# Hybrid encoder trunk on one core: small constants merged or moved, S5 eigenvalues first, silu(c) as a row in its own stream

## The chip, the cores and the metric

The kernel runs on one core of a Trainium2 chip. The metric is the device time of one execution in microseconds (us). A run that times a kernel repeats it; the median of the repeats counts. One further execution was recorded by the hardware profiler, and all rows below come from that one.

## The reference, cut to what matters

Two encoder layers are applied to x (512 tokens by 2048 channels, f32), both conditioned on a vector c (2048).

```python
def ada_modulate(x, c, norm_g, ada_w, ada_b):
    mod = silu(c) @ ada_w + ada_b                   # 2048 -> 3 * 2048
    shift, scale, gate = split(mod, 3)
    return rms_norm(x, norm_g) * (1 + scale) + shift, gate

# layer 0
h, gate = ada_modulate(x, c, ...)
q, k, v, g_a, u, g_b = split(h @ w_in)
out = concat(attention(q, k, v) * silu(g_a), s5(u) * silu(g_b)) @ w_out
x = x + gate * out
# layer 1: the same wrapper round a neighbourhood attention and an SSD scan
```

The S5 part needs tables of powers of its eigenvalues (lambda, log step, and a vector of the exponents), the matrices B and C, a diagonal D, and a gated output projection with a bias. All products are f32, built of three passes on a split into a rounded high part and a rest.

## The kernel before, in words

All loads and stores are issued from one queue, SP's. A planner of the kernel framework fixes the order of the instructions on every engine's queue before the run, from the program's order, from priorities (`high_priority`), from when it thinks that each one's inputs are ready, and from `issue_after(ins)`, which keeps an instruction behind another on the same queue without a wait. A load that the program asks for late, but whose buffer is free, can thus stand very early in SP's queue.

`setup` (L905) loads x in eight pieces of 512 KB (L909), then calls `silu_c` (L589), which loads c twice, as columns (`cs`) and as rows (`c_row`), applies silu to both (L599 to L601), and writes the rows to a scratch in DRAM, `cbd` (L602). Then come the identity matrix `ident` (L912) and `mods` (L923), the columns of norms and biases. `s5_params` (L267) loads the eigenvalues `s5_lam` (L277) and the exponents `s5_kx` (L278) and computes the S5 tables step by step, mostly on VectorE (L282 to L361).

`layer0` (L925) then runs 16 rounds k, one for each block of 128 input channels. A round needs four quarters of the adaLN weights, 512 KB each, for block k (`ada_load`, L939, into OLa for even and OLb for odd k) and a 384 KB piece of the input projection (`w_issue`, L142). `ada_sum` (L973, L978, L980) forms shift and scale on TensorE, `ada_cols` (L987 to L992) applies them to x that `x_norm` (L1000) has multiplied by the reciprocal root `rstd` (L651 to L655, from the squares L952 and the sums L956). Then 18 matmuls of the u projection follow (L167 to L169), from round 4 on also 24 of `extra`, with another 512 KB of weights (`w_x`). The quarters of round k + 2 are loaded into the buffer that `ada_sum(k)` has read. `ada_sum(k + 1)` writes the same PSUM bank (b3) from which `ada_cols(k)` reads.

```python
def load_after(self, k):
    return self.tc.issue_after(self.adal[k].ins) if k in self.adal else nullcontext()
```

The S5 matrices C (L498, L499) are queued behind the adaLN quarters of round 4, B (L367) behind those of round 14. Once C is there, the S5 tables of 512 KB each are formed on VectorE (L393 to L397) and written to DRAM (L410).

Later streams run beside the matmuls of the projections, advanced a step at a time by `slot`. `ada_stream` (L604) forms the other modulation vectors on VectorE from 512 KB pieces (L615) and from silu(c), read back from `cbd` and spread over the partitions into `cb` (L624). Small constants are loaded where they are used in the program: `s5dd` (L508, L509) in `s5_kernels`, `bglu` (L1133; scaled on ScalarE, L1134 and L1135) before the GLU matmuls, `tri` and `ssd_rows` (L1201, L1202), `convw` (L1307, scaled on ScalarE L1310), `ssdw` (L1474, scaled on ScalarE L1476), `wqk` (L1499, used on VectorE L1502).

Of the kernel before, what the change touches and what calls it, by code (L numbers as in the profile page):

```python
# [12 lines left out]
AF = mybir.ActivationFunctionType  # L13
ALU = mybir.AluOpType
# [11 lines left out]
HEAD = 1  # L26
PRI_B = 3000
NZ = 6
LK = (-1, 14)
SSLOT = 2  # L30
WB = 3
N0 = 4
# [34 lines left out]
class Trunk:  # L67
# [69 lines left out]
    def w_issue(self, upto, offset=PRI_WD):  # L137
        while self.wi < min(upto, len(self.wq)):
            src = self.wq[self.wi]
            t = self.sl("w", src.shape, bufs=2)  # L140
            with self.tc.high_priority(offset=offset):
                self.wd[self.wi] = self.nc.sync.dma_start(out=t, in_=src)  # L142
            self.wf[self.wi] = t
            self.wi += 1

    def w_prep(self, upto):
        while self.wp < min(upto, len(self.wq)):
# [119 lines left out]
    def s5_params(self, tr, keep, ks):  # L267
# [3 lines left out]

        nc, A = self.nc, self.A
        ev = nc.vector
        w = self.sl(tr[0], [128, 11, 64])
        kx = self.sl("s5kx", [128, 16])
        with self.load_after(ks[0]):
            nc.sync.dma_start(out=w[:, 0:3], in_=A["s5_lam"])  # L277
            nc.sync.dma_start(out=kx, in_=A["s5_kx"])  # L278
        yield
        yield  # L280
        lr, li, dt = w[:, 0], w[:, 1], w[:, 3:11]
        nc.scalar.activation(out=dt[:, 0], in_=w[:, 2], func=AF.Exp)  # L282
        yield
        ev.tensor_tensor(out=dt[:, 1], in0=lr, in1=dt[:, 0], op=ALU.mult)
        ev.tensor_tensor(out=dt[:, 2], in0=li, in1=dt[:, 0], op=ALU.mult)
# [10 lines left out]
        x = self.sl(tr[2], [128, 16, 64])  # L296
# [3 lines left out]
        for c in range(2):  # L300
# [7 lines left out]
            t = self.sl(tr[3], [128, 16, 64])  # L308
# [53 lines left out]
        bb = [self.sl(keep[2 + c], [128, 1024]) for c in range(2)]  # L362
        self.s5_bb = bb
        bt = [self.sl(tr[4 + c], [128, 1024]) for c in range(2)]
        with self.load_after(ks[1]):
            for c in range(2):
                nc.sync.dma_start(out=bt[c], in_=A["s5_b"][:, c])  # L367
        yield
        yield
        for half in range(2):  # L370
            g = slice(half * 32, half * 32 + 32)
# [130 lines left out]
    def s5_kernels(self, ts):  # L502


        nc, A = self.nc, self.A
        self.s5_kk = self.scratch("s5_kk", [16, 128, 240])
        dd = self.sl("s5dd", [128, 2, 16])
        nc.sync.dma_start(out=dd[:, 0], in_=A["s5_dcol"])  # L508
        nc.sync.dma_start(out=dd[:, 1], in_=A["s5_dmask"])  # L509
        w = self.sl(ts[3], [128, 4, 240])  # L510
        cks = {i: self.s5_load_ck(ts[i], i) for i in range(3)}
        yield
        for i in range(16):
# [12 lines left out]
            yield  # L526
            ks = w[:, i % 4]
            nc.scalar.copy(out=ks[:, 0:128], in_=kv[1])
            nc.scalar.copy(out=ks[:, 128:240], in_=kv[0][:, 16:128])
            nc.vector.scalar_tensor_tensor(out=ks[:, 112:128], in0=dd[:, 1], scalar=dd[:, 0, i:i + 1],  # L530
                                           in1=ks[:, 112:128], op0=ALU.mult, op1=ALU.add)
            nc.vector.tensor_tensor(out=ks[:, 112:128], in0=ks[:, 112:128], in1=kv[0][:, 0:16], op=ALU.add)
            nc.sync.dma_start(out=self.s5_kk[i], in_=ks)
            yield
# [51 lines left out]
                nc.sync.dma_start(out=ydram[:, (j - 1) * 4:(j + 1) * 4], in_=y)  # L586
            yield

    def silu_c(self):  # L589

        nc, A = self.nc, self.A
        self.cs = self.sl("cs", [128, 16])
        self.cbd = self.scratch("cbd", [16, 128])
        cr = self.sl("rsq", [16, 2, 128])
        t = self.sl("cst", [128, 16])
        nc.sync.dma_start(out=self.cs, in_=A["c"])
        nc.sync.dma_start(out=cr[:, 0], in_=A["c_row"])
        for x, w in ((self.cs, t), (cr[:, 0], cr[:, 1])):
            nc.scalar.activation(out=w, in_=x, func=AF.Tanh, scale=0.5)  # L599
            nc.vector.scalar_tensor_tensor(out=x, in0=w, scalar=1.0, in1=x, op0=ALU.add, op1=ALU.mult)  # L600
            nc.vector.tensor_scalar(out=x, in0=x, scalar1=0.5, scalar2=None, op0=ALU.mult)  # L601
        nc.sync.dma_start(out=self.cbd, in_=cr[:, 0])  # L602

    def ada_stream(self, groups, tags):  # L604

# [298 lines left out]

    def setup(self):  # L905
        nc, A = self.nc, self.A
        self.xt = [self.sl(f"G{i}", [128, 2, 512]) for i in range(8)]
        for i in range(8):
            nc.sync.dma_start(out=self.xt[i], in_=A["x"].rearrange("(j k p) s -> j p k s", k=2, p=128)[i])  # L909
        self.silu_c()  # L910
        self.ident = self.sl("ident", [128, 128])
        nc.sync.dma_start(out=self.ident, in_=A["ident"])  # L912
        self.ones = self.sl("ones", [128, 1])
        nc.vector.memset(self.ones, 1.0)
        self.epsc = self.sl("epsc", [128, 1])
        nc.vector.memset(self.epsc, EPS)

        self.quad = self.sl("quad", [128, 1])
        nc.vector.tensor_reduce(out=self.quad, in_=self.ident.rearrange("p (a b) -> p b a", b=32)[:, 0], axis=AX.X,
                                op=ALU.add)  # L920

        self.mods = self.sl("mods", [128, 128])
        nc.sync.dma_start(out=self.mods, in_=A["mods"])  # L923

    def layer0(self):  # L925
        nc, A = self.nc, self.A
# [148 lines left out]
        def s5_rest():  # L1075
            yield from self.s5_in([G[14], G[3], G[1], G[2], G[15], G[16], G[17]], st)
            yield from self.qk_tables(("ropeq", "ropek"), G[8])
            a, b = self.s5_scan(st), self.s5_kernels(G[14:18])
            la = lb = True
            while la or lb:  # L1080
                la = la and next(a, "end") != "end"
                lb = lb and next(b, "end") != "end"
                yield
            yield from self.s5_out([G[14], G[15], G[3], G[16], G[10], G[17], G[11], G[0], G[2], G[1]], st, ydram)
        self.start("s5", s5_rest())
        self.sstep = SSLOT
        extra(17)
# [45 lines left out]
        nc.sync.dma_start(out=bglu[:, 0], in_=A["bglu"])  # L1133
# [61 lines left out]
    def dt_stream(self, raw, G):  # L1195
# [2 lines left out]
        v = nc.vector  # L1198
        tri = self.sl(G[13], [128, 3, 128])
        self.tri = tri  # L1200
        nc.sync.dma_start(out=tri[:, 0:2], in_=A["tri"])  # L1201
        nc.sync.dma_start(out=tri[:, 2, 0:80], in_=A["ssd_rows"])  # L1202
# [100 lines left out]
    def conv_stream(self, xins, G, xs):  # L1303

        nc, A = self.nc, self.A
        cw = self.sl("convw", [128, 12, 6])
        nc.sync.dma_start(out=cw, in_=A["convw"])  # L1307
        yield
        yield
        nc.scalar.mul(out=cw, in_=cw, mul=0.5)  # L1310
# [151 lines left out]
    def ssd_end(self, G, ys, z):  # L1462
# [11 lines left out]
        nc.sync.dma_start(out=nw, in_=self.A["ssd_nw"])  # L1474
        yield
        nc.scalar.mul(out=nw, in_=nw, mul=0.5)  # L1476
        for t in range(4):
# [15 lines left out]
    def na_stream(self, T, raws, oc, gdram):  # L1493
# [2 lines left out]
        A = self.A  # L1496
        v = nc.vector
        wqk = self.sl("wqk", [128, 2])
        nc.sync.dma_start(out=wqk, in_=A["o_qkn"])  # L1499
# [321 lines left out]
def host_s5(I):  # L1821
    f = {}
    lre, lim, ls = (np.asarray(I[k])[0] for k in ("s5_lam_re", "s5_lam_im", "s5_log_step"))
    ls = np.broadcast_to(ls[:, :, None], (2, 64, 64))
    f["s5_lam"] = np.stack([a.transpose(0, 2, 1).reshape(128, 64) for a in (lre, lim, ls)], axis=1)
# [7 lines left out]
    for g in range(4):  # L1833
        o = 16 * (g % 2)
        at[0, g, o:o + 16], at[1, g, o:o + 16] = d[g], e[g]
    f["s5_dcol"], f["s5_dmask"] = at.reshape(2, 128, 16)
    j = np.arange(8, dtype=np.float32)
    f["s5_kx"] = np.concatenate([np.repeat(np.concatenate([j + 1, j])[None], 64, 0),
                                 np.repeat(np.concatenate([8 - j, 7 - j])[None], 64, 0)])
    return f  # L1840


def host_layer0(I):
    f = {}
    a = lambda n: np.asarray(I[n])
    f["x"] = a("x")[0].T
    f["c"] = a("c")[0].reshape(16, 128).T
    f["c_row"] = a("c")[0].reshape(16, 128)
    f["ident"] = np.eye(128, dtype=np.float32)
    col = lambda v: v.reshape(16, 128).T  # L1850
    eb, obb = a("e_ada_b")[0], a("o_ada_b")[0]
    f["mods"] = np.concatenate(
        [col(v) for v in (a("e_norm_g")[0], a("o_norm_g")[0], eb[4096:], obb[:2048], obb[2048:4096], obb[4096:],
                          eb[:2048], eb[2048:4096])], axis=1)
# [125 lines left out]
```

## Time and profile before

| | us |
|---|---|
| median of 3 runs | 1838.96 |
| the 3 runs | 1835.25 to 1839.21 |
| the profiled execution's own time | 1831.32 |
| its span, first to last instruction | 1829.5 |
| TensorE busy | 1770.3 (97%) |
| VectorE busy | 1209.7 (66%) |
| ScalarE busy | 730.0 (40%) |
| granted TensorE clock, mean | 0.992 |

Busy is the time in which the engine had at least one instruction running. The time outside the span is 1.8 us. DMA share is the mean busy share of the 16 DMA engines in a stretch (records overlap, so it can read a little over 1), and GB/s is what they moved.

### The profile page before, as it was taken

What the parts mean: (1) busy time and instruction counts of PE and PEld (TensorE: products, weight loads), DVE (VectorE), ACT (ScalarE), POOL (GpSimd) and SP (SyncE); (2) the same over time, 40 slices, a digit from 0 to 9 for tenths busy, and PEclk for the clock granted to TensorE, in tenths of its full rate; (3) what the DMA queues carried; (4) which work ended last, traced back from release to release, by engine and by line L of the source; (5) the groups of instructions that cost most, each with busy time, mean ns of one, the idle gap of its engine ahead of it and who ended that gap; (6) DMA issues with size and microseconds to landing.
All of it is one profiled execution on the core that took longest, in us unless ns stands there. A gap on an engine that the chain in (4) does not pass through costs nothing.

```text
span 1829.5 us, 28824 instructions
## 1 busy us (share of the span) xinstructions
PE 1770.3 (97%) x11176; PEld 1522.8 (83%) x11176; DVE 1209.7 (66%) x2336; ACT 730.0 (40%) x1357; POOL 25.1 (1%) x44
## 2 busy tenths in 40 slices
PE   6899999899999989999999999999999999999999
PEld 3677897699989867888878878878799999997887
DVE  6897697984699999842256676589974453644332
ACT  6333454236235434432243244356644343442211
POOL 0000000000000000011100000000000000000000
PEclk8999999999999989999999999999999999999999
DMA  9997626747989887664435743358533333243542
GB/s 325 375 340 278 186 79 220 241 124 247 313 315 295 285 283 259 209 207 140 138 108 161 246 142 117 104 169 250 165 105 115 110 99 102 93 141 100 180 140 90
DMA packets 140906, 347.52 MB, mean 190 GB/s; under 512 B 31488, under 2 KB 42656, under 8 KB 140768
## 3 DMA queue, kind: packets, MB, share of 16 engines
q1 hardware_dynamic: 140768, 345.67, 57.6%
q8 instruction: 88, 1.44, 0.3%
q14 instruction: 50, 0.41, 0.1%
HBM read 310.48 MB, written 33.56 MB: 188 GB/s over the span
## 4 chain that ended last, share of the span: by engine, by line
PE 65%; DVE 16%; DMA 12%; issue 3%; ACT 1%; SPq 1%; DVEq 0%; ACTq 0%
PE m L167 10%; PE m L169 10%; PE m L168 10%; PE m L235 7%; PE m L234 7%; PE m L236 7%; DMA G<-in_ada_r_dram 6%; DVE G L629 3%; DVE wl L129 3%; PE b L169 2%; PE b L167 2%; PE b L168 2%; PE b L573 1%; PE b L973 1%; PE b L461 1%
## 5 line engine op out<-in xcount | busy, mean ns | idle before, releaser
L129 DVE TENSOR_TENSOR wl<-w,wh 128x1024 fp32r<-128x1024 f32 (+2 forms) x262 | 313.9, 1199 | 256.8 <-ACT wh L128 254.0
L128 ACT CAST wh<-w 128x1024 fp32r<-128x1024 f32 (+2 forms) x262 | 269.1, 1029 | 522.3 <-PE m L168 267.5
L168 PE MATMUL m<-H,wh 128*128 128x512 f32 (+1 forms) x968 | 381.9, 395 | 1.2 <-DVE H L992 1.2
L167 PE MATMUL m<-H,wh 128*128 128x512 f32 (+1 forms) x968 | 380.8, 398 | 2.2 <-ACT G L1144 2.1
L169 PE MATMUL m<-H,wl 128*128 128x512 f32 (+1 forms) x968 | 378.8, 396 | 2.2 <-DVE wl L129 2.2
L234 PE MATMUL m<-wh,H 128*128 128x256 f32 (+2 forms) x1232 | 353.3, 288 | 2.6 <-ACT H L665 1.5
L236 PE MATMUL m<-wh,H 128*128 128x256 f32 (+2 forms) x1232 | 353.8, 289 | 0.3 <-DVE H L1765 0.3
L235 PE MATMUL m<-wl,H 128*128 128x256 f32 (+2 forms) x1232 | 353.0, 287 | 0.2 <-DVE wl L129 0.2
L234 PEld LDWEIGHTS m<-wh,H 128*128 128x128 f32 x1232 | 233.8, 190 | 7.3 <-ACT H L665 2.6
L236 PEld LDWEIGHTS m<-wh,H 128*128 128x128 f32 x1232 | 233.4, 190 | 3.5 <-issue 1.0
L235 PEld LDWEIGHTS m<-wl,H 128*128 128x128 f32 x1232 | 234.0, 190 | 2.6 <-issue 0.7
L167 PEld LDWEIGHTS m<-H,wh 128*128 128x128 f32 x968 | 182.9, 190 | 46.0 <-issue 4.2
L169 PEld LDWEIGHTS m<-H,wl 128*128 128x128 f32 x968 | 181.8, 188 | 44.1 <-issue 3.5
L168 PEld LDWEIGHTS m<-H,wh 128*128 128x128 f32 x968 | 182.3, 188 | 42.4 <-issue 2.6
L629 DVE SCALAR_TENSOR_TENSOR G<-G,cb 128x1024 f32<-128x1024 f32 x128 | 155.0, 1220 | 55.5 <-DMA G<-in_ada_r_dram 47.7
L169 PE MATMUL m<-OLa,wl 128*128 128x512 f32 (+1 forms) x132 | 51.3, 389 | 0.6 <-DVE wl L129 0.5
L167 PE MATMUL m<-OLa,wh 128*128 128x512 f32 (+1 forms) x132 | 51.5, 390 | 0.2 <-ACT wh L128 0.2
L167 PE MATMUL m<-OLb,wh 128*128 128x512 f32 (+1 forms) x132 | 50.1, 388 | 1.4 <-ACT OLb L128 1.4
L167 PE MATMUL b<-H,wh 128*128 128x512 f32 x128 | 50.2, 406 | 0.8 <-DVE G L1045 0.8
L169 PE MATMUL m<-OLb,wl 128*128 128x512 f32 (+1 forms) x132 | 50.9, 386 | 0.0
L168 PE MATMUL m<-OLa,wh 128*128 128x512 f32 (+1 forms) x132 | 50.8, 385 | 0.0
L168 PE MATMUL m<-OLb,wh 128*128 128x512 f32 (+1 forms) x132 | 50.7, 384 | 0.0
(406 smaller groups left out, 2685.2 us busy)
## 6 DMA issues: line engine op xcount, KB each, us to landing
G<-in_ada_r_dram SPq DMA_DIRECT2D x128, 512.0 KB
w<-in_w_kvq_dram SPq DMA_DIRECT2D x72, 512.0 KB
w<-in_w_out_dram SPq DMA_DIRECT2D x64, 512.0 KB
w<-in_w_x_dram SPq DMA_DIRECT2D x36, 512.0 KB
OLa<-in_ada_dram SPq DMA_DIRECT2D x32, 512.0 KB
OLb<-in_ada_dram SPq DMA_DIRECT2D x32, 512.0 KB
G<-s_ck SPq DMA_DIRECT2D x32, 512.0 KB
s_ck<-G SPq DMA_DIRECT2D x16, 512.0 KB
```

The costliest lines, as they stand in the source:

```text
L128: self.nc.scalar.copy(out=hi, in_=src)
L129: self.nc.vector.tensor_tensor(out=lo, in0=src, in1=hi.bitcast(F32), op=ALU.subtract)
L167: mm(out=out, lhsT=lh, rhs=rh, start=start, stop=False)
L168: mm(out=out, lhsT=lh, rhs=rl, start=False, stop=False)
L169: mm(out=out, lhsT=ll, rhs=rh, start=False, stop=stop)
L234: mm(out=o, lhsT=hi, rhs=wh[:, c], start=(k == 0 and i % per == 0), stop=False)
L235: mm(out=o, lhsT=hi, rhs=wl[:, c], start=False, stop=False)
L236: mm(out=o, lhsT=lo, rhs=wh[:, c], start=False, stop=last)
L461: nc.tensor.matmul(out=xp[c][:, gg * 64:gg * 64 + 64], lhsT=gt[:, c, g], rhs=self.s5_u(b * 4 + g))
L573: nc.tensor.matmul(out=yp[:, cols], lhsT=ck[:, c, g], rhs=sts[:, j % 2, c, g], start=False, stop=(c == 1))
L629: nc.vector.scalar_tensor_tensor(out=t, in0=t, scalar=1.0, in1=cb, op0=ALU.mult, op1=ALU.mult, accum_out=o)
L973: nc.tensor.matmul(out=ps[32 * i:32 * i + 32, 0:256], lhsT=self.cs[:, 4 * q + i:4 * q + i + 1].to_broadcast([128, 32]), rhs=abuf[k][:, q, ...
```

## The change

Constants that go together become one input each: identity, `mods` and c as columns are one block of 272 columns, `consts`; the S5 eigenvalues and exponents are one block of 208 columns, `s5_lamk`; the two halves of `s5dd` are one. `s5_lamk` is loaded before anything else, `consts` between the fifth and the sixth piece of x. The silu of c as rows, its store to `cbd` and so the first `cb` move into a stream `silu_row` that starts with the S5 stream after the 16 rounds. `late()` queues a load behind the weight piece issued last in the program: `c_row`, `s5dd`, `bglu`, `tri`, `ssd_rows`, `convw`, `ssdw` and `wqk` get it.

```diff
+    def late(self):
+        return self.tc.issue_after(self.wd[self.wi - 1].ins)
...
 def s5_params
-        w = self.sl(tr[0], [128, 11, 64])
-        kx = self.sl("s5kx", [128, 16])
-        with self.load_after(ks[0]):
-            nc.sync.dma_start(out=w[:, 0:3], in_=A["s5_lam"])
-            nc.sync.dma_start(out=kx, in_=A["s5_kx"])
+        w = self.s5w
...
 def s5_kernels
-        nc.sync.dma_start(out=dd[:, 0], in_=A["s5_dcol"])
-        nc.sync.dma_start(out=dd[:, 1], in_=A["s5_dmask"])
+        with self.late():
+            nc.sync.dma_start(out=dd, in_=A["s5_dd"])
...
-    def silu_c(self):
...
-        nc.sync.dma_start(out=self.cs, in_=A["c"])
-        nc.sync.dma_start(out=cr[:, 0], in_=A["c_row"])
...
+    def silu_row(self):
...
+        with self.late():
+            nc.sync.dma_start(out=cr[:, 0], in_=self.A["c_row"])
+        yield
+        yield
+        self.silu(cr[:, 0], cr[:, 1])
+        yield
         nc.sync.dma_start(out=self.cbd, in_=cr[:, 0])
+        yield
...
 def setup
+        self.s5w = self.sl("G14", [128, 768])
+        nc.sync.dma_start(out=self.s5w[:, 0:208], in_=A["s5_lamk"])
...
+        consts = self.sl("consts", [128, 272])
+        self.ident, self.mods, self.cs = consts[:, 0:128], consts[:, 128:256], consts[:, 256:272]
         for i in range(8):
+            if i == 5:
+                nc.sync.dma_start(out=consts, in_=A["consts"])
             nc.sync.dma_start(out=self.xt[i], in_=...)
-        self.silu_c()
-        nc.sync.dma_start(out=self.ident, in_=A["ident"])
+        self.silu(self.cs, self.sl("cst", [128, 16]))
...
-        nc.sync.dma_start(out=self.mods, in_=A["mods"])
...
 def layer0, after the 16 rounds
+        self.start("crow", self.silu_row())
         self.start("s5", s5_rest())
...
 bglu (and tri, ssd_rows, convw, ssdw, wqk in the same way)
+        with self.late():
+            nc.sync.dma_start(out=bglu[:, 0], in_=A["bglu"])
```

## Rows read from the trace of the kernel before

**Rows 1.** The page's head and its busy table.
```profile
span 1829.5 us, 28824 instructions
PE 1770.3 (97%) x11176; PEld 1522.8 (83%) x11176; DVE 1209.7 (66%) x2336; ACT 730.0 (40%) x1357; POOL 25.1 (1%) x44
```

**Rows 2.** Stretches: length, then busy time of each engine, clock, DMA share, GB/s.
```profile
13.00:20.00 7.00, 5.41 (x26) 1.73 (x24) 6.01 (x17) 6.20 (x11) 0.00 (x0) 1.00 0.92 299
28.00:35.00 7.00, 7.00 (x39) 4.86 (x32) 6.97 (x12) 4.11 (x10) 0.00 (x0) 0.69 0.68 192
35.00:64.00 29.00, 21.76 (x170) 14.87 (x172) 18.93 (x41) 13.46 (x28) 0.00 (x0) 0.98 1.02 401
64.00:70.00 6.00, 6.00 (x38) 3.51 (x36) 6.00 (x11) 2.73 (x4) 0.00 (x0) 0.51 1.01 383
70.00:190.00 120.00, 119.12 (x764) 87.78 (x763) 104.39 (x177) 42.86 (x60) 0.43 (x2) 1.00 0.83 305
200.00:300.00 100.00, 99.44 (x683) 87.58 (x684) 74.58 (x127) 53.50 (x85) 0.00 (x0) 1.00 0.47 133
300.00:400.00 100.00, 91.19 (x926) 75.81 (x912) 96.75 (x337) 24.76 (x51) 0.00 (x0) 1.00 0.63 200
```

**Rows 3.** SP's queue in order of time: start, us, line, transfer, count.
```profile
0.73 4.08 SPq L909 DMA_DIRECT2D G<-in_x_dram  x8
4.86 0.47 SPq L596 DMA_DIRECT2D cs<-in_c_dram  x1
...
11.52 0.33 SPq L278 DMA_DIRECT2D s5kx<-in_s_kx_dram  x1
12.87 2.62 SPq L939 DMA_DIRECT2D OLa<-in_ada_dram  x4
...
19.62 0.33 SPq L142 DMA_DIRECT2D w<-in_w_u_dram  x1
20.89 0.33 SPq L508 DMA_DIRECT2D s5dd<-in_s_dcol_dram  x1
...
28.36 0.32 SPq L602 DMA_DIRECT2D cbd<-rsq  x1
29.28 2.79 SPq L939 DMA_DIRECT2D OLa<-in_ada_dram  x4
...
35.27 0.52 SPq L624 DMA_DIRECT2D cb<-cbd  x1
...
43.48 0.33 SPq L498 DMA_DIRECT2D G<-in_s_c_dram  x1
46.02 0.33 SPq L142 DMA_DIRECT2D w<-in_w_u_dram  x1
```

**Rows 4.** The chain that ended last, 40 to 70 us: start, us, what.
```profile
45.52 0.81 issue
...
53.26 0.49 issue
...
60.38 3.48 issue
63.86 3.64 PE b L973 x32
```

**Rows 5.** VectorE in order of time, in two stretches.
```profile
17.13 2.34 DVE L290 TENSOR_TENSOR G<-G,s5kx 128x1024 f32<-128x1024 f32 x2
...
23.61 0.67 DVE L655 SCALAR_TENSOR_TENSOR r2k<-H,H 128x512 f32<-128x512 f32 x1
...
60.46 0.69 DVE L393 TENSOR_TENSOR H<-G,G 128x512 f32<-128x512 f32 x1
...
63.48 0.22 DVE L987 SCALAR_TENSOR_TENSOR acols<-b,mods 128x1 f32<-128x1 f32 x1
```

**Rows 6.** A GLU weight piece: its issue on SP, its first use on ScalarE.
```profile
614.48 0.33 SPq L142 DMA_DIRECT2D w<-in_w_glu_dram  x1
620.22 1.05 ACT L128 CAST wh<-w 128x1024 fp32r<-128x1024 f32 x1 [1.33 <-DMA w<-in_w_glu_dram]
```

More of the change, by code (lines that the diff above doesn't have):

```diff
@@ L28 @@
 NZ = 6
-LK = (-1, 14)
+LK = 14
 SSLOT = 2
@@ L273, in s5_params @@
         ev = nc.vector
-        w = self.sl(tr[0], [128, 11, 64])
-        kx = self.sl("s5kx", [128, 16])
-        with self.load_after(ks[0]):
-            nc.sync.dma_start(out=w[:, 0:3], in_=A["s5_lam"])
-            nc.sync.dma_start(out=kx, in_=A["s5_kx"])
+        w = self.s5w
         yield
         yield
-        lr, li, dt = w[:, 0], w[:, 1], w[:, 3:11]
-        nc.scalar.activation(out=dt[:, 0], in_=w[:, 2], func=AF.Exp)
+        kx = w[:, 192:208]
+        lr, li, dt = w[:, 0:64], w[:, 64:128], w[:, 256:768].rearrange("p (a g) -> p a g", g=64)
+        nc.scalar.activation(out=dt[:, 0], in_=w[:, 128:192], func=AF.Exp)
         yield
@@ L364, in s5_params @@
         bt = [self.sl(tr[4 + c], [128, 1024]) for c in range(2)]
-        with self.load_after(ks[1]):
+        with self.load_after(ks):
             for c in range(2):
@@ L587, in s5_out, with silu @@
             yield
-    def silu_c(self):
-        nc, A = self.nc, self.A
-        self.cs = self.sl("cs", [128, 16])
+    def silu(self, x, w):
+        nc = self.nc
+        nc.scalar.activation(out=w, in_=x, func=AF.Tanh, scale=0.5)
+        nc.vector.scalar_tensor_tensor(out=x, in0=w, scalar=1.0, in1=x, op0=ALU.add, op1=ALU.mult)
+        nc.vector.tensor_scalar(out=x, in0=x, scalar1=0.5, scalar2=None, op0=ALU.mult)
+    def silu_row(self):
+        nc = self.nc
         self.cbd = self.scratch("cbd", [16, 128])
         cr = self.sl("rsq", [16, 2, 128])
-        t = self.sl("cst", [128, 16])
-        nc.sync.dma_start(out=self.cs, in_=A["c"])
-        nc.sync.dma_start(out=cr[:, 0], in_=A["c_row"])
[L598 to L601, printed above, removed]
+        with self.late():
[4 more added lines that the diff above has]
+        yield
         nc.sync.dma_start(out=self.cbd, in_=cr[:, 0])
+        yield
     def ada_stream(self, groups, tags):
@@ L920, in setup @@
                                 op=ALU.add)
-        self.mods = self.sl("mods", [128, 128])
-        nc.sync.dma_start(out=self.mods, in_=A["mods"])
     def layer0(self):
@@ L1132, in layer0 @@
         bglu = self.sl("bglu", [128, 2, 16])
-        nc.sync.dma_start(out=bglu[:, 0], in_=A["bglu"])
+        with self.late():
+            nc.sync.dma_start(out=bglu[:, 0], in_=A["bglu"])
         nc.scalar.mul(out=bglu[:, 1], in_=bglu[:, 0], mul=0.25)
@@ L1200, in dt_stream @@
         self.tri = tri
-        nc.sync.dma_start(out=tri[:, 0:2], in_=A["tri"])
-        nc.sync.dma_start(out=tri[:, 2, 0:80], in_=A["ssd_rows"])
+        with self.late():
+            nc.sync.dma_start(out=tri[:, 0:2], in_=A["tri"])
+            nc.sync.dma_start(out=tri[:, 2, 0:80], in_=A["ssd_rows"])
         bias, alog, dd = tri[:, 2, 0:32], tri[:, 2, 32:64], tri[:, 2, 64:80]
@@ L1306, in conv_stream @@
         cw = self.sl("convw", [128, 12, 6])
-        nc.sync.dma_start(out=cw, in_=A["convw"])
+        with self.late():
+            nc.sync.dma_start(out=cw, in_=A["convw"])
         yield
@@ L1473, in ssd_end @@
         nw = self.sl("ssdw", [128, 8])
-        nc.sync.dma_start(out=nw, in_=self.A["ssd_nw"])
+        with self.late():
+            nc.sync.dma_start(out=nw, in_=self.A["ssd_nw"])
         yield
@@ L1498, in na_stream @@
         wqk = self.sl("wqk", [128, 2])
-        nc.sync.dma_start(out=wqk, in_=A["o_qkn"])
+        with self.late():
+            nc.sync.dma_start(out=wqk, in_=A["o_qkn"])
         yield
@@ L1824, in host_s5 @@
     ls = np.broadcast_to(ls[:, :, None], (2, 64, 64))
-    f["s5_lam"] = np.stack([a.transpose(0, 2, 1).reshape(128, 64) for a in (lre, lim, ls)], axis=1)
+    lam = np.concatenate([a.transpose(0, 2, 1).reshape(128, 64) for a in (lre, lim, ls)], axis=1)
     b = [np.asarray(I[k])[0].transpose(0, 2, 1, 3).reshape(128, 1024) for k in ("s5_b_re", "s5_b_im")]
@@ L1835, in host_s5 @@
         at[0, g, o:o + 16], at[1, g, o:o + 16] = d[g], e[g]
-    f["s5_dcol"], f["s5_dmask"] = at.reshape(2, 128, 16)
+    f["s5_dd"] = at.reshape(2, 128, 16).transpose(1, 0, 2)
     j = np.arange(8, dtype=np.float32)
-    f["s5_kx"] = np.concatenate([np.repeat(np.concatenate([j + 1, j])[None], 64, 0),
-                                 np.repeat(np.concatenate([8 - j, 7 - j])[None], 64, 0)])
+    kx = np.concatenate([np.repeat(np.concatenate([j + 1, j])[None], 64, 0),
+                         np.repeat(np.concatenate([8 - j, 7 - j])[None], 64, 0)])
+    f["s5_lamk"] = np.concatenate([lam, kx], axis=1)
     return f
@@ L1846, in host_layer0 @@
     f["x"] = a("x")[0].T
-    f["c"] = a("c")[0].reshape(16, 128).T
     f["c_row"] = a("c")[0].reshape(16, 128)
-    f["ident"] = np.eye(128, dtype=np.float32)
     col = lambda v: v.reshape(16, 128).T
     eb, obb = a("e_ada_b")[0], a("o_ada_b")[0]
-    f["mods"] = np.concatenate(
-        [col(v) for v in (a("e_norm_g")[0], a("o_norm_g")[0], eb[4096:], obb[:2048], obb[2048:4096], obb[4096:],
-                          eb[:2048], eb[2048:4096])], axis=1)
+    f["consts"] = np.concatenate(
+        [np.eye(128, dtype=np.float32)] + [col(v) for v in (a("e_norm_g")[0], a("o_norm_g")[0], eb[4096:], obb[:2048], obb[2048:4096], obb[4096:],
+                          eb[:2048], eb[2048:4096], a("c")[0])], axis=1)
     e0, o0 = a("e_ada_w")[0], a("o_ada_w")[0]
```

1 line of the change is left out of this document (removed).

## The prediction

> **What bounds the kernel now.** Read the page's head first: TensorE is busy for 1770.3 of 1829.5 us [rows 1], so 59 us of the span are without a matmul, and a change that touches no matmul can win only there or where the clock is low. The stretches say where that is. From 35 to 64 us TensorE works 21.76 of 29.00 us while the DMA engines are full (share 1.02, 401 GB/s); from 64 to 70 it is busy but at clock 0.51, the level of 1.2 GHz; from 70 to 190 it is busy for 119.12 of 120.00 us with DMA at 0.83, and from 200 to 300 for 99.44 of 100.00 [rows 2]. So the first 64 us are bound by loads, what follows by TensorE, and a load that lands sooner matters until about 64 us.
>
> SP's queue shows how the loads are fed. The eight pieces of x go out in 4.08 us; from there on an issue follows every 1.3 us or so: the loads of 4.86 to 12.87 us are six small ones and the first adaLN quarter, 8.01 us for six steps [rows 3]. 1.33 us is what 512 KB take at 401 GB/s (1.31): each issue waits until the transfer eight places ahead of it has landed. Eight transfers are under way, whatever their size, and when most of them are small the engines run dry. This is seen twice in the stretches: at 13 to 20 us they move 299 GB/s, after the six small loads, and at 28 to 35 us 192, after the seven from 20.89 to 28.36 us, which stand between the weights of round 1 and the quarters of round 2 [rows 2, 3].
>
> The chain of waits in 40 to 70 us shows what TensorE does meanwhile: it waits 0.81 us and 0.49 us at the ends of rounds, then 3.48 us before `ada_sum(5)`, which then runs in 3.64 us at the low clock [rows 4]. The three waits grow as the loads fall behind.
>
> **The change part by part.** All sums are against the profiled execution's 1831.32 us, which is 1.8 us around the span and stands 7.6 us under the median of the three runs (1838.96); the difference found there is carried over to the median.
>
> *The two holes close.* In front of the quarters of round 0 now stand big pieces and two blocks of 104 and 136 KB; between the weights of round 1 and the quarters of round 2 stands nothing. Quarters of round 2 need `ada_sum(0)` done, but behind it a whole round of loads is still under way, so the queue stays full. Against 401 GB/s the holes cost 7.00 x (401 - 299) / 401 = 1.8 us and 7.00 x (401 - 192) / 401 = 3.6 us [rows 2]: 5.4 us.
>
> *`cb` and the small bytes leave.* `cb` (512 KB) goes out at 35.27 us, inside the full stretch. By the rule of eight, the issue at 46.02 us is the one that waited for it, 2.54 us after the one at 43.48 instead of 1.3 [rows 3]. At the full rate its bytes cost 1.3 us, by that spacing at most 2.54; I take 1.5, near the bytes, since other transfers go on meanwhile. The other small loads are 73 KB, 0.2 us.
>
> *What comes in front.* The eigenvalues are issued before x: 4.08 / 8 = 0.5 us of SP's queue ahead of every load. The two blocks hold the bytes that were there before, now ahead of x's end: the last piece of x comes 0.5 + 240 KB / 401 GB/s = 1.1 us later, the quarters behind it 0.5.
>
> Together the loads up to round 5 land 5.4 + 1.5 + 0.2 - 0.5 = 6.6 us sooner.
>
> *VectorE's S5 steps.* With the eigenvalues there at 3 us instead of after 11.52, the first steps run between the squares of x. Now they stand in the way: the pair L290 holds VectorE for 2.34 us from 17.13, and `rstd` ends at 23.61 + 0.67 [rows 5]. The start of the first u matmuls should gain 2 to 3 us in spite of the later x. This adds nothing to the sum while TensorE waits for loads in each round; it makes room: TensorE has 35 to 64 us with 7.2 us idle, so a lead of 6.6 us does not yet make it the bound.
>
> *The clock.* The 6.00 us at 0.51 cost 6.00 x 0.49 = 2.9 us [rows 2]. They follow the wait of 3.48 us; the waits of 0.81 and 0.49 us left the clock at 0.98 in the mean [rows 2, 4]. If TensorE starts 2 to 3 us earlier and the loads come 6.6 us earlier, the waits of four rounds shrink to some 3.5 us in all, below 1 us each, near the short ones. I take the whole 2.9; the other end is 0.
>
> *What is late next.* VectorE: `acols` of round 4 ran at 63.48 us behind a row of S5 steps that began at 60.46 [rows 5], and `ada_sum(5)` needs the bank that it frees. The quarters of round 5 landed just then too, so the row cannot tell which of the two ended the wait. If the planner leaves such a row of steps there, up to 63.48 - 60.46 = 3.0 us of the gain stay away, if not, none; with no row to decide, I take half, 1.5.
>
> *The silu row and `cb`, after round 15.* Three transfers (`c_row`, `cbd`, `cb`), three small operations and two landings that SP waits for in order, now among the S5 loads of u. What hides them is TensorE's queue, 99.44 of 100.00 us, beside a DMA share of 0.47 [rows 2]. Without that cover the price is what `cb` cost at 43.48, 2.54 us [rows 3]. I take 0.
>
> *The late loads* (`s5dd`, `bglu`, `tri`, `ssd_rows`, `convw`, `ssdw`, `wqk`) wait in stages that are not bound by loads. I take 0; the third rival prices them. Merging itself takes instructions from SP's queue alone, which is idle most of the time.
>
> Sum: -6.6 - 2.9 + 1.5 = -8.0 us, from 1831.32 to 1823.3; on the median 1838.96 - 8.0 = **1831.0**.
>
> By rows a small load costs 5.4 us / 13 = 0.4 us in the full stretch. The Trainium skill, "DMA: Bandwidth & Descriptors", in the part on the two cost components, has each transfer pay a fixed 2.0 us or so, mostly for its completion; twelve transfers fewer before 40 us would by that be worth an estimate of 24 us if they came one after another. The rows contradict such a sum, since eight are under way at a time, and I keep to them.
>
> **The rivals.**
>
> *Loads lead, VectorE follows.* VectorE takes over as the bound of the rounds: it is busy for 104.39 of 120.00 us in 70 to 190, and for 96.75 of 100.00 in 300 to 400, the S5 scan [rows 2]. If each round waits for steps put ahead of `acols`, the wait of 3.0 us and the low clock after it stay and the lead is cut again later: 6.6 - 3.0 = 3.6 us at most, and 0 at worst, 1835 to 1839. For it speaks the row of steps before 63.48; against it that S5 work moves into the idle VectorE of the first 15 us, and that TensorE was not held from 70 to 190.
>
> *The change does not open the queue.* The planner may put other loads whose buffers are free into the gap, or keep the weights of round 2 waiting for VectorE's split, so that the next quarters stand behind them: no gain, 1838 to 1840. Against it: after these thirteen the queue holds only loads that need buffers still in use.
>
> *Slower, by late constants on ScalarE.* `bglu`, `convw` and `ssdw` are scaled on ScalarE (L1134, L1310, L1476), now soon after their issue. If ScalarE's queue reaches one before it has landed, the weight casts behind it wait, and TensorE behind those. A load among busy queues takes, as the GLU piece shows, 620.22 - 614.48 = 5.74 us from issue to use [rows 6]; three full waits are 17.2 us, and with the gain of 8.0 the kernel would be 9.2 us slower, 1848. It decides from 8.0 + 3.7 = 11.7 us of waiting on, that is, two of the three in full. For it: ScalarE works through its queue in order. Against it: weights are split two pieces ahead, so TensorE has work for most of such a wait. The Trainium skill, "DMA: Bandwidth & Descriptors", among its rules for kernel authors, advises issuing a load early and waiting for it late; the change does the reverse for seven constants, and by that rule this rival is the one to expect; no row here shows such a late constant yet.
>
> **How the numbers follow.** 0.2% is 3.7 us, about what a measurement of this kernel can tell from no change. The forecast, 5 to 11 us faster, has 0.62. VectorE as the bound has 0.19, of which a quarter still gains over 3.7 us; the unopened queue 0.08, which is no change; late constants 0.11, slower. Faster is 0.62 + 0.05 = 0.67, no change 0.14 + 0.08 = 0.22, slower 0.11. The range: with 2.54 for `cb`, no steps in the way and the whole clock it is 6.6 + 1.0 + 2.9 = 10.5 us, 1828.5; the three runs shown reach 3.7 us under their median, so 1825 is the low end. The high end takes in no change, 1840. Left out are most of the late constants and a little below.
>
> **What would show it.** Right: at 13 to 35 us the DMA engines stay at some 400 GB/s; SP issues the quarters of round 2 some 5 us before 29.28; `ada_sum(5)` starts at about 57 us at the full clock; the 16 rounds end 8 us sooner, and so does each later stage. Wrong: TensorE still waits 3 us before round 5, now for `acols`; a wait at L1134, L1310 or L1476 with weight casts behind it; a new gap between 200 and 300 us behind `cb`; or a lead that is there at the end of the rounds and gone at the end of the S5 stream.

## The result and the profile of the changed kernel

The changed kernel takes 1846.85 us (median of 7 runs, 1842.01 to 1852.55), the kernel before in the same comparison 1835.25 (7 runs, 1830.19 to 1839.21). The ratio is 1.0063, interval 1.0041 to 1.0085: 11.6 us slower, where 8 us faster was forecast. The profiled execution took 1843.35 us, that of before 1831.32.

The page's head and busy table of the changed kernel:

```profile
span 1841.6 us, 28798 instructions
PE 1784.2 (97%) x11176; PEld 1532.5 (83%) x11176; DVE 1208.6 (66%) x2336; ACT 729.3 (40%) x1356; POOL 25.2 (1%) x44
```

Against [rows 1] TensorE's time without a matmul has not grown: 1841.6 - 1784.2 = 57.4 us, before 59.2. The mean granted clock has fallen from 0.992 to 0.987: 1784.2 x 0.013 = 23.2 us lost to it, before 1770.3 x 0.008 = 14.2. These two account for -1.8 + 9.0 = 7.2 of the 12.1 us between the profiles. Stretches show where (columns as in [rows 2]):

```profile
13.00:20.00 7.00, 6.77 (x19) 2.31 (x19) 7.00 (x14) 5.05 (x9) 0.00 (x0) 1.00 1.04 406
28.00:35.00 7.00, 6.88 (x42) 4.00 (x34) 6.22 (x14) 3.81 (x16) 0.00 (x0) 0.87 1.02 402
60.00:64.00 4.00, 2.99 (x25) 1.40 (x26) 4.00 (x9) 2.47 (x3) 0.00 (x0) 0.57 0.59 131
200.00:300.00 100.00, 100.00 (x696) 88.07 (x694) 74.60 (x136) 53.40 (x89) 0.00 (x0) 1.00 0.50 137
300.00:400.00 100.00, 95.30 (x908) 79.03 (x908) 96.07 (x331) 23.20 (x47) 0.00 (x0) 0.95 0.60 192
400.00:480.00 80.00, 77.96 (x562) 73.90 (x562) 35.10 (x65) 44.70 (x84) 0.00 (x0) 0.94 0.72 230
650.00:800.00 150.00, 133.98 (x662) 110.07 (x661) 126.94 (x261) 63.32 (x122) 0.14 (x2) 0.95 0.74 238
```

The same two late stretches of the kernel before:

```profile
400.00:480.00 80.00, 79.99 (x609) 75.81 (x609) 42.83 (x80) 45.71 (x84) 0.00 (x0) 1.00 0.78 248
650.00:800.00 150.00, 139.28 (x696) 115.46 (x695) 127.00 (x253) 62.12 (x119) 0.27 (x4) 0.97 0.73 238
```

The first two rows: the holes are closed, 406 and 402 GB/s where [rows 2] had 299 and 192. From 200 to 300 us nothing is lost. Count as lost the time without a matmul plus busy time times what the clock lacks. From 650 to 800 us (the attention and the GLU) that is 16.0 + 134.0 x 0.05 = 22.7 us, before 10.7 + 139.3 x 0.03 = 14.9; from 300 to 480 us 4.7 + 4.8 + 2.0 + 4.7 = 16.2, before 8.8. SP's queue (start, us, line, transfer, count) and the chain of waits (start, us, what):

```profile
15.14 2.95 SPq L949 DMA_DIRECT2D OLb<-in_ada_dram  x3
19.05 0.33 SPq L142 DMA_DIRECT2D w<-in_w_u_dram  x1
20.39 3.85 SPq L949 DMA_DIRECT2D OLa<-in_ada_dram  x4
```

```profile
57.50 3.51 issue
61.01 2.79 PE b L983 x24
```

The quarters of round 2 go out at 20.39, 8.9 us before [rows 3]. The wait before `ada_sum(5)` is 3.51 us, as in [rows 4], and comes 2.9 us earlier. VectorE shows why it stays:

```profile
58.56 1.29 DVE L395 TENSOR_TENSOR G<-G,G 128x512 f32<-128x512 f32 x2
59.77 0.95 DVE L129 TENSOR_TENSOR wl<-w,wh 128x768 fp32r<-128x768 f32 x1
60.63 0.21 DVE L997 SCALAR_TENSOR_TENSOR acols<-b,consts 128x1 f32<-128x1 f32 x1
```

`acols` again stands behind a row of S5 steps and, now, a weight split [rows 5]. Here it was not the loads that ended the wait: the last quarter of round 5 had gone out at 47.19 us, and before 61.01 nearly nothing is under way, since SP's next issue, at 60.75, comes when that split has ended (60.72).

```profile
60.00:61.00 1.00, 0.00 (x0) 0.02 (x1) 1.00 (x4) 0.05 (x1) 0.00 (x0) 0.77 0.13 53
```

The S5 scan, one line of VectorE, before, then in the changed kernel (durations min/median/max in ns, then first and last start):

```profile
L483 DVE TENSOR_TENSOR w2k<-OLa,s5lt x62: 358/378/406, 263.6 to 400.9; 128x128 f32<-128x128 f32 x62
```

```profile
L484 DVE TENSOR_TENSOR w2k<-OLa,s5lt x62: 360/382/401, 258.2 to 397.0; 128x128 f32<-128x128 f32 x62
```

It begins 5.4 us ahead and ends 3.9 ahead. The output projection's evictions, before, then in the changed kernel:

```profile
L1176 DVE SCALAR_TENSOR_TENSOR G<-m,mods,G x17: 484/751/752, 799.0 to 941.5; 128x512 f32<-128x512 f32 x15, 128x256 f32<-128x256 f32 x2
```

```profile
L1188 DVE SCALAR_TENSOR_TENSOR G<-m,consts,G x17: 484/751/752, 808.4 to 953.0; 128x512 f32<-128x512 f32 x15, 128x256 f32<-128x256 f32 x2
```

The first comes at 808.4 us, before at 799.0: 9.4 us behind. So the front gained what it was to gain, roughly, and the loss lies between. VectorE in the changed kernel at the first large wait of the 650-to-800 stretch, then ScalarE, then TensorE:

```profile
661.68 1.22 DVE L636 SCALAR_TENSOR_TENSOR G<-G,cb 128x1024 f32<-128x1024 f32 x1
...
662.82 1.22 DVE L636 SCALAR_TENSOR_TENSOR G<-G,cb 128x1024 f32<-128x1024 f32 x1
...
663.97 0.69 DVE L843 TENSOR_REDUCE sst<-b 128x1 f32<-128x512 f32 x1
664.57 1.22 DVE L636 SCALAR_TENSOR_TENSOR G<-G,cb 128x1024 f32<-128x1024 f32 x1
...
665.71 0.69 DVE L843 TENSOR_REDUCE sst<-b 128x1 f32<-128x512 f32 x1
666.32 1.22 DVE L129 TENSOR_TENSOR wl<-w,wh 128x1024 fp32r<-128x1024 f32 x1
```

```profile
660.83 1.05 ACT L128 CAST wh<-w 128x1024 fp32r<-128x1024 f32 x1 [5.34 <-PE m L172]
```

```profile
667.59 0.50 PE L173 MATMUL m<-H,wl 128*128 128x512 f32 x1 [3.65 <-DVE wl L129]
```

The high half of a GLU weight piece is ready at 661.88. VectorE splits off the low half (L129) at 666.32, behind three steps of the modulation stream (L636, 1.22 us each; they can stand much later, as e13 below shows) and two reductions, and TensorE stands for 3.65 us. The two longest of TensorE's waits in 640 to 800 us:

```profile
PE b L171 <- ACT G L846: 4.0, 1, 4.0
PE m L173 <- DVE wl L129: 3.6, 1, 3.6
```

The longer one, at 686.27, is put down to ScalarE, but ScalarE's L846 had itself waited 3.55 us for VectorE's L844 (685.04), which stands behind three more steps of L636 (679.14, 680.88, 683.90). The kernel before has one wait of this size there, 4.4 us for another split on VectorE.

### The profile page after: what moved, and what is told of

Read it like the earlier page. It is cut to its first block, busy times and chain, and to the rows that moved or that the text cites. A ratio compares the mean times of both kernels' runs of the same rounds, so it can differ in the third digit from the quotient of the medians.

```text
span 1841.6 us, 28798 instructions
## 1 busy us (share of the span) xinstructions
PE 1784.2 (97%) x11176; PEld 1532.5 (83%) x11176; DVE 1208.6 (66%) x2336; ACT 729.3 (40%) x1356; POOL 25.2 (1%) x44
## 4 chain that ended last, share of the span: by engine, by line
PE 67%; DVE 14%; DMA 12%; issue 3%; ACT 2%; SPq 1%; DVEq 0%; ACTq 0%
PE m L171 10%; PE m L173 10%; PE m L172 10%; PE m L238 7%; PE m L240 7%; PE m L239 7%; DMA G<-in_ada_r_dram 6%; DVE G L636 3%; PE b L173 2%; PE b L171 2%; PE b L172 2%; DVE wl L129 2%; PE b L983 2%; PE b L462 1%; DMA G<-csd 1%
## 5 line engine op out<-in xcount | busy, mean ns | idle before, releaser
L129 DVE TENSOR_TENSOR wl<-w,wh 128x1024 fp32r<-128x1024 f32 (+2 forms) x262 | 314.6, 1202 | 261.5 <-ACT wh L128 258.2
L636 DVE SCALAR_TENSOR_TENSOR G<-G,cb 128x1024 f32<-128x1024 f32 x128 | 155.3, 1228 | 68.2 <-DMA G<-in_ada_r_dram 59.9
```

What stands on the lines that cost most here:

```text
L129: self.nc.vector.tensor_tensor(out=lo, in0=src, in1=hi.bitcast(F32), op=ALU.subtract)
L636: nc.vector.scalar_tensor_tensor(out=t, in0=t, scalar=1.0, in1=cb, op0=ALU.mult, op1=ALU.mult, accum_out=o)
```

## The experiments

The theories, as the expectations call them. **A**: the late constants, `s5dd` above all, arrive too late. **B**: the planner orders all queues anew when loads move, and TensorE's waits fall elsewhere, far from the edit. **C**: the work of the silu row and `cb`, put behind the 16 rounds, costs the time itself. Each kernel was timed in five rounds beside the kernel before, on the same chip. "Moved" compares the order of VectorE's instructions in the traces: of the 465 that the kernel before has between 480 and 850 us, it counts the fewest that have to change their place to give the run's order. "Lead" is the first start of the S5 scan against 263.6 us, in one profile each; the changed kernel's two profiles have 5.4 and 3.5.

| run | what | lead, us | moved | ratio, 95% interval |
|---|---|---|---|---|
| e1 | front alone | 0.6 | 0 | 1.0003 (0.9993 to 1.0014) |
| e2 | front, late constants | 1.6 | 0 | 0.9997 (0.9986 to 1.0009) |
| e3 | front, row stream | 2.4 | 51 | 1.0031 (1.0014 to 1.0048) |
| e4 | all, loads at piece 21 | 4.9 | 0 | 0.9978 (0.9967 to 0.9989) |
| e5 | all, row as a call | 0.5 | 0 | 1.0017 (1.0003 to 1.0031) |
| e6 | e5, constants at piece 15 | 0.5 | 0 | 1.0011 (0.9997 to 1.0026) |
| e7 | row stream late, constants at 15 | 5.5 | 178 | 1.0060 (1.0041 to 1.0079) |
| e8 | the changed kernel again | 3.5 | 178 | 1.0041 (1.0028 to 1.0054) |
| e9 | changed, `c_row` at piece 29 | 2.5 | 0 | 1.0011 (0.9995 to 1.0027) |
| e10 | all at piece 23 | 4.5 | 0 | 0.9979 (0.9964 to 0.9994) |
| e11 | all at piece 25 | 2.8 | 235 | 1.0047 (1.0027 to 1.0068) |
| e12 | changed, `c_row` at piece 21 | 3.2 | 0 | 0.9987 (0.9972 to 1.0001) |
| e13 | changed, modulation steps held | 4.1 | 293 | 0.9924 (0.9899 to 0.9949) |
| e14 | all at piece 9 | -0.2 | 58 | 1.0009 (0.9994 to 1.0024) |
| e15 | all at piece 19 | 2.6 | 0 | 0.9986 (0.9973 to 0.9999) |
| e16 | changed, one store first | 6.2 | 178 | 1.0047 (1.0030 to 1.0063) |
| e17 | e10, modulation steps held | 3.7 | 275 | 0.9906 (0.9888 to 0.9924) |
| e18 | before, modulation steps held | -0.1 | 275 | 0.9920 (0.9905 to 0.9936) |

**One part at a time (e1 to e4).** e1 takes `late()` and the row's stream out of the changed kernel, e2 only the stream, e3 only `late()`; e4 keeps all of it, with the anchor bounded:

```diff
 def late
-        return self.tc.issue_after(self.wd[self.wi - 1].ins)
+        return self.tc.issue_after(self.wd[min(self.wi - 1, 20)].ins)
```

> Front alone: eigenvalues first, the blocks consts and s5_lamk; no late() anywhere, silu row and cbd in setup as before. Theory A (late constants: s5dd issued at 308.55 us holds the S5 kernel stream, first s_kk store 313.0 instead of 296.0, and bglu and others later; that is where the lead of 4 to 6 us goes): no loss after 300 us, 3 to 6 us faster than before (about 1830), first s_kk store near 293. Theory B (the planner writes another order with any edit, and stalls and low clock fall elsewhere, whichever part is changed): anything from 5 us faster to 12 us slower, with waits at places that neither trace shows. Theory C (the silu row and cb as a stream cost it): 3 to 6 us faster.

> Front and late(), silu row and cbd in setup as before. Theory A: as slow as after, 8 to 12 us over before, first s_kk store near 313, the wait of TensorE behind the eviction L581 near 446 and the low clock after it there again. Theory B: between 5 us faster and 12 us slower. Theory C: 3 to 6 us faster than before.

> Front and silu row as a stream, but late() does nothing (the planner puts c_row and the small constants near the front of SP's queue itself). Theory A: 2 to 6 us faster than before, first s_kk store near 293. Theory B: between 5 us faster and 12 us slower. Theory C: 8 to 12 us slower.

> The whole change, but late() queues the constants behind the 21st weight piece (about 100 us) where the program asks for them later: off the front, and there long before their use. Theory A: the lead of 6 us is kept to the end, 5 to 8 us faster than before (about 1828), s_kk first store near 291. Theory B: between 6 us faster and 12 us slower, whatever the first s_kk store. Theory C: 8 to 12 us slower.

e2 speaks against A: with `s5dd` as late as in the changed kernel (the first `s_kk` store at 317 us, before at 296) it costs nothing. e3 speaks against A too: its constants are early again, and it is slower all the same. e4 is faster than before: `c_row`, `cbd` and `cb` out of the front, constants off it, the lead kept. On C it says little, since its row stands at 152.66 to 170.74 us (`c_row` to `cb`), ahead of the loads of u. Against C speaks the changed kernel itself: its row stands at 211.39 to 218.73 us, and TensorE is busy there without a gap (the row 200 to 300 us above). The front by itself (e1) brings nothing while `c_row`, `cbd` and `cb` stand in it.

**The row as a call, and as a stream (e5 to e8).** In e5 and e6 `self.silu_row()` is a plain call where `self.start("crow", self.silu_row())` stood; e6 and e7 have the constants, not `c_row`, bounded at piece 15; e8 is the changed kernel.

> The whole change, but the silu row is written out as a plain call where the stream was started (after the 16 rounds, no yields between its steps): the same loads, the same work, about the same place. Theory B (order: behind some 250 us the order of VectorE's instructions is that of the front-and-late kernel, without the orders at 650 to 850 us that the row as a stream brings): the front's lead of 4 to 6 us stays to the end, 2 to 6 us faster than before, some 1832, TensorE's waits at 664, 682 and 782 us gone. Theory C (the row's own work and its cb after the rounds cost it): as slow as after, 6 to 12 us over before. Theory A (the late constants cost it): 4 to 12 us over before, with the loss between 300 and 470 us.

> The same as the run with the row as a plain call, and the constants s5dd, bglu, convw, wqk, ssdw, tri queued behind the 15th weight piece (about 75 to 130 us) at the latest. Theory B: 3 to 7 us faster than before, some 1831; the s_kk stores begin near 291 us. Theory A: this one 5 to 7 us faster than before and 6 us or more faster than the one with the row as a call and late constants. Theory C: 6 to 12 us slower than before.

> As the run before it (constants behind the 15th weight piece), but the silu row as a stream again, as in after. Theory B: 4 to 9 us slower than the one with the row as a plain call, lost between 480 and 850 us in TensorE's waits for VectorE's weight splits and for ScalarE's exponentials, 1835 to 1840. Theory C: as slow as the one with the row as a call. Theory A: 5 us faster than before.

> The changed kernel itself once more, on the same chip as the three variants of it: 1842 to 1849, 0.4 to 0.8% over before; a second profile shows whether the waits at 446, 664, 682 and 782 us stand where they stood (all theories: yes, since the order of the instructions is fixed; the low clock behind each may differ).

e7 against e6 is B's case: the same loads and work, and 0.5% slower, with 178 moved. But e5 and e6 are not faster than before, which B had expected; here C has a small part. SP's queue in e5, then the wait that follows:

```profile
202.11 0.43 SPq L424 DMA_DIRECT2D G<-udram  x1
202.58 0.44 SPq L605 DMA_DIRECT2D cbd<-rsq  x1
206.23 0.34 SPq L627 DMA_DIRECT2D cb<-cbd  x1
206.67 0.38 SPq L1028 DMA_DIRECT2D udram<-G  x1
207.14 0.38 SPq L142 DMA_DIRECT2D w<-in_w_gb_dram  x1
210.96 4.25 SPq L424 DMA_DIRECT2D G<-udram  x9
```

```profile
217.42 3.14 PE L462 MATMUL b<-G,G 128*128 128x64 f32 x16 [1.90 <-DMA G<-udram]
```

`cb` stands on the queue until its store `cbd` has landed, 206.23 - 203.02 = 3.2 us, and holds a store of u behind it (206.67). The loads of u wait for that store and go on at 210.96, in e10 at 206.55. TensorE waits 1.90 us and runs at the low clock afterwards (0.76 in the mean of 220 to 230 us); the lead, 6.6 us at the 19th weight cast (144 us), is 0.5 at the scan. In the changed kernel `cb` stands behind all loads of u (218.73) and this wait does not occur. e8 has the changed kernel's waits near 664, 682 and 782 us again (3.23, 4.01 and 1.77 us), but not the one at 446.

**The anchor alone (e9 to e12).** e10 and e11 are e4 with 22 and 24 for 20; e9 and e12 bound `c_row` alone, at 28 and 20.

> The changed kernel in which only c_row is queued earlier: behind the 29th weight piece instead of the one issued last (some 30 us earlier); all other constants late as in after, the silu row a stream as in after. Theory B (after some 220 us VectorE's order is that of the front-and-late kernel again, not that of after): S5 scan begins 5 us before that of the kernel before and the lead is kept, 2 to 6 us faster than before, 1831 to 1835. Theory C (silu row and cb as work after the front cost the time): as slow as after, 6 to 12 us over before. Theory A (late constants): slower than before by 3 us or more.

> The whole change, all late constants and c_row behind the 23rd weight piece at the latest (the run with the 21st took 1832.6). Theory B, and A and C too: as that one, 2 to 6 us faster than before; the order behind 250 us is the same as there.

> The same with the 25th weight piece instead of the 23rd: the same loads some 10 us later, far from any use. The order of the instructions behind 230 us is another one (on VectorE some thousand of 2210 instructions stand elsewhere). Theory B: 3 us or more off the run with the 23rd piece, on either side, with TensorE waits between 300 and 850 us that are not there with the 23rd. Theories A and C: the same time as with the 23rd piece, within 2 us.

> The changed kernel in which only c_row is queued behind the 21st weight piece; s5dd, bglu, convw, tri, ssdw, wqk late as in after. Theory B: 2 to 6 us faster than before, as the run with all constants behind the 21st piece (1832.6). Theory A: 3 us or more slower than that run, so no faster than before. Theory C: 2 to 6 us faster than before.

e10 and e11 differ in one digit: six small loads, and the row's two transfers behind them, go out some 7 us later. The first of them, `c_row`, in e10, then in e11:

```profile
165.41 0.42 SPq L603 DMA_DIRECT2D rsq<-in_c_row_dram  x1
```

```profile
173.04 0.42 SPq L603 DMA_DIRECT2D rsq<-in_c_row_dram  x1
```

The order behind them is another one, and the times are 1834.09 and 1845.30 us, 0.7% apart. From 70 to 300 us, where these transfers stand, TensorE is without a matmul for 2.0 us more in e11; the rest is lost later, so it is not mainly the loads' own cost. e9 and e12 leave the constants late: 1.0011 and 0.9987, so A is worth little (e12 against e10: 0.1%, less than the intervals can tell). e9 is a miss for B: none moved, and not faster than before. Its row stands among the loads of u (`cbd` at 195.37, `cb` at 197.61), and TensorE waits 1.2 us for one of them, as in e5. But `c_row` alone, queued 58 us earlier (e12, 153.15 us), takes over 0.5% off the changed kernel, though no work is saved.

Of the kernels without the hold that follows, the nine with none moved have ratios of 0.9978 to 1.0017, the five with 51 to 235 moved, e14 apart, 1.0031 to 1.0060; e14, with 58, has 1.0009. From 650 to 800 us TensorE loses, counted as above, 13.6 to 19.9 us in the nine, 19.1 to 24.9 in the five, 16.0 in e14.

**Intervening in the order (e13 to e18).** e13's edit only says where VectorE's modulation steps may stand while the GLU's weights are split:

```diff
 def w_prep
-                self.split(hi, lo, t)
+                self.lsp = self.split(hi, lo, t)
 def ada_stream
+            with self.tc.issue_after(self.lsp.ins) if 76 <= self.wp < 92 else nullcontext():
-            nc.vector.scalar_tensor_tensor(out=t, ... accum_out=o)
+                nc.vector.scalar_tensor_tensor(out=t, ... accum_out=o)
```

> The changed kernel in which, while the weights of the GLU are split (pieces 76 to 91), each step of the modulation stream on VectorE is kept behind the low half (L129) of the weight piece that is split last in the program. Theory B: TensorE's wait of 3.2 to 3.7 us near 663 us, which stood behind four modulation steps of 1.22 us on VectorE, is gone; the stretch from the first GLU gate to the first output eviction falls from 182 to 184 us to 178 or less, the whole by 3 us or more against after. Theory C (the time is bound by VectorE's work there, in whatever order): the wait comes back in another place, the stretch and the whole within 2 us of after, or longer.

> The whole change, all late constants and c_row behind the 9th weight piece at the latest. The order of VectorE's instructions against the run with the 23rd piece differs before 250 us and, from 719 to 810 us, in some 170 instructions. Theory B: the stretch from 720 to 850 us is 4 to 8 us longer than with the 23rd piece, and the whole 3 to 8 us slower, 1837 to 1842. Theory C: the same time as with the 23rd piece, within 2 us, 1834.

> The same behind the 19th weight piece: the order behind 230 us is that of the runs with the 21st and the 23rd. All theories: as those two, 0.2% faster than before, 1831 to 1834.

> The changed kernel with one store of the S5 output (ydram, near 443 us) two places earlier on SP's queue, ahead of two loads of s_kk; nothing else moves. Theory B: ScalarE's wait for that store near 443 us is 1 to 2 us shorter, so that TensorE's wait near 446 us is there in no profile; the whole 1 to 3 us faster than after, mostly by the low clock that follows such a wait. Rival (that wait is one of several and the lead is gone anyway): within 1 us of after.

> Both: late constants and c_row behind the 23rd weight piece at the latest, and the modulation steps held behind the weight splits of the GLU. Theory B (the lead of the front is 4 to 5 us at the start of the S5 scan; what took it were waits that the order made): 0.8 to 1.1% faster than before, 1816 to 1821, and 3 to 6 us faster than the kernel before with the hold alone. Rival (the front's lead is lost in any case, somewhere behind the scan): within 2 us of the kernel before with the hold alone.

> The kernel before with the modulation steps held behind the weight splits of the GLU, nothing else. Theory B: its 18 us of TensorE's excess time between 650 and 800 us fall to 2 or so, 0.6 to 0.9% faster than before, 1820 to 1826; 2 us either side of the changed kernel with the hold (1823), if what the change lost lay in that stretch, and 4 to 6 us faster than it, if it lay elsewhere.

e13 takes 1823.22 us, 22 to 24 less than the changed kernel in its two timings. The hold gives all engines another order, but nearly only between 480 and 850 us: e18 against before has 275 of VectorE's instructions moved there and one elsewhere, and 483 of TensorE's 2078 matmuls there. The 650-to-800 stretch of e13, of e17 and of e18, one row each:

```profile
650.00:800.00 150.00, 150.00 (x730) 125.31 (x729) 120.88 (x199) 59.85 (x93) 4.57 (x5) 1.00 0.76 267
```

```profile
650.00:800.00 150.00, 150.00 (x726) 125.20 (x725) 121.70 (x201) 60.34 (x93) 4.57 (x5) 1.00 0.78 272
```

```profile
650.00:800.00 150.00, 150.00 (x731) 125.28 (x730) 121.80 (x202) 59.65 (x93) 4.56 (x5) 1.00 0.77 272
```

TensorE is without a matmul for not one moment of it and the clock is full, in all three. VectorE is busy for 121 to 122 us, not much less than 127: the work was not too much for it, the order made TensorE wait. The steps run to 928 us instead of 789, and part of the gain is given back: from 800 to 950 us e13 loses 9.3 us, the kernel before 2.6. e18's first eviction of the output projection comes at 772.6 us, 26 ahead of before, and its median is 14 us lower. e18 shows where most of the loss lay: with the hold, the kernel before (0.9920) and the changed one (0.9924) are equal within their intervals, so about all that the change lost was in the order of 480 to 850 us that the hold replaces. But the lead of the front does not show in e13 either: 4.1 us at the first step of the scan, 1.1 at the last, and its first eviction comes at 773.5 us, 0.9 behind e18's. Where it went is open. e17, with the front's lead as well, has 0.9906; that it is faster than e18 the intervals don't show, so this part of its expectation stays open. e17 and e18 beat both kernels.

e14 is 5.5 us slower than e10, as B said, but not where B had it: from 720 to 850 us TensorE loses 2.2 us, in e10 1.2, where 4 to 8 us more were expected. Its lead is gone at the scan already, and from there to the first eviction the two take the same time (537.6 and 538.1 us). e15 has e10's order and its time. e16 is a miss for B: the store goes out earlier, TensorE's wait at 446 us is gone, as it is in e8 without the edit, and the time is that of the changed kernel.

## Why the prediction was wrong

**What held.** The holes closed at about 400 GB/s, and the quarters of round 2 came 8.9 us sooner (some 5 forecast). TensorE's loss up to 70 us, time without a matmul and low clock, fell from 18.9 + 51.1 x 0.12 = 25.0 to 17.0 + 53.0 x 0.05 = 19.6 us.

**What was mis-sized.** The wait before `ada_sum(5)` did not go: 3.51 us, for `acols`, the mechanism of the first rival; 1.5 us had been kept for it, and the prediction could not tell which of loads and VectorE ended it. The low clock was won in part; it follows that wait at 0.57 from 60 to 64 us. Where the later order stays (e4, e10), the front is worth 4.5 to 4.9 us at the scan, and 0.2% or 4 us by the ratios (the medians lie 3.8 and 1.6 us under before): half of the 8.0 forecast or less. And it needs the row out of the front: e1, without that, has 0.6.

**What failed: the two parts taken at 0.** The silu row and `cb` after round 15, and the late loads, were costed as transfers, each by what hides it. By that measure 0 was near the truth for the constants: e12 has them late and loses to e10 no more than 0.1%, within the intervals. But the step assumed that the rest of the program stays as it is. In the changed kernel the order between 480 and 850 us was another one, on VectorE (178 of 465 instructions) and with it on TensorE (332 of 2078 matmuls), though of the moved loads only `bglu` falls into it, and from 650 to 800 us it cost 22.7 - 14.9 = 7.8 us; the second profile of the changed kernel gives 14.5 + 135.5 x 0.06 = 22.7 as well. With no instruction moved there it was 13.6 to 19.9. The 7.8 us are more than the 5.4 won in front. The prediction even read the planner's order as the cause of the row of steps before 63.48, and did not ask what a moved load does to it elsewhere. It also read [rows 2] to 400 us only: the 150 us in which TensorE loses most, behind VectorE's order, stood in no part of it.

The rest of the loss does not lie in one place. The profile shows 7.4 us from 300 to 480 us, most of it the wait at 446 us and the low clock after it; the second profile has neither. Of the 12.1 us between the profiles 4.9 are in busy TensorE time at the full clock and remain unexplained; what TensorE's own new order costs was not tested. Why the planner's order flips at piece 25 and not at 23 was not followed.

**The rivals.** "Slower, by late constants on ScalarE" had the right sign and the wrong cause. ScalarE in the changed kernel, at `ssdw` and at `convw`:

```profile
1396.90 0.21 ACT L1491 ACTIVATE ssdw<-ssdw 128x8 f32<-128x8 f32 x1 [4.92 <-DMA ssdw<-in_ssd_nw_dram]
```

```profile
1063.88 0.26 ACT L1324 ACTIVATE convw<-convw 128x72 f32<-128x72 f32 x1 [1.04 <-DMA convw<-in_convw_dram]
```

`bglu` is not waited for. Together 5.96 us, half of the 11.7 from which it was to decide, and TensorE works from 1390 to 1400 us and from 1055 to 1066 without a gap. So the advice that the prediction cited, from the Trainium skill, "DMA: Bandwidth & Descriptors", its rules for kernel authors, to issue early and wait late, does not bear on this result: the loads that come late are waited for by an engine that has time. The fixed 2.0 us that the prediction took from the same page of the Trainium skill is there a fit for transfers issued from GpSimd; those here go out from SP, and no run here isolates such a cost. "The change does not open the queue" fell at once.

## What to carry to other kernels

Where a planner fixes the order of queues, an edit of a few loads is two edits: its own, and a new order behind it; compare the instruction lists of the two programs before pricing the first, and test a neighbouring position of the same loads (here 0.7% apart) before believing either sign. Look for the stretch in which TensorE loses most, whether the change touches it or not, and see whether work that is needed late stands ahead of a weight split there; keeping it behind by hand was worth 0.8%, more than the change was ever to bring.

## What the runs showed of the hardware

Some waits, and the low clock after a wait, are a matter of the single execution. The same program, two profiles, at 450 us (the changed kernel, then its repeat):

```profile
446.00:450.00 4.00, 2.08 (x15) 1.95 (x16) 0.34 (x1) 2.83 (x5) 0.00 (x0) 0.96 0.76 247
450.00:460.00 10.00, 10.00 (x41) 9.42 (x42) 2.54 (x4) 4.61 (x8) 0.00 (x0) 0.50 0.32 103
```

```profile
446.00:450.00 4.00, 4.00 (x38) 4.00 (x37) 0.68 (x2) 2.92 (x5) 0.00 (x0) 1.00 0.95 322
450.00:460.00 10.00, 10.00 (x71) 9.19 (x69) 4.54 (x7) 4.60 (x8) 0.00 (x0) 1.00 0.46 129
```

A wait of 1.86 us, behind a ScalarE instruction that had waited 4.1 us for a store, was followed by 10 us at clock 0.50, the level of 1.2 GHz, in one profile; the other has neither the wait nor the low clock. It cost 1.9 us and half of the 10. Near 782 us both profiles have the same wait before the same matmul, 1.88 and 1.77 us; the stretches behind it:

```profile
784.00:788.00 4.00, 3.37 (x21) 2.99 (x22) 1.55 (x3) 1.55 (x3) 0.00 (x0) 1.00 0.80 266
```

```profile
782.50:786.00 3.50, 3.04 (x15) 3.00 (x15) 2.32 (x5) 1.58 (x3) 0.00 (x0) 0.51 0.73 281
```

In the first the clock stayed full, in the second it fell to 0.51. Runs of one kernel spread over some 10 us here, and one profile is no measure of 0.2%.
